# Starting the expert stage beside the routing of the last token tile

## The chip, the cores and the metric

The kernel runs on one core of a Trainium2 chip. The metric is device microseconds of one execution. Its engines work side by side and meet at semaphores: PE (TensorE, matrix products and transposes), DVE (VectorE), ACT (ScalarE), POOL (GpSimd) and SP, which here only issues transfers. POOL issues the transfers whose rows are picked by an index list (gathers and scatters). All transfers share 16 DMA engines.

## The reference, cut to what matters

One decoder layer over 1024 prompt tokens and 32 sample tokens: two kinds of attention, an output projection, then a mixture of 32 experts of which each token takes two.

```python
h = x + mixed @ w_out
f = hier_moe(rms_norm(h, g_ffn).reshape(B * T, -1), w_rg, b_rg, w_re, b_re, w_g, w_u, w_d)
return h + f.reshape(B, T, -1)

def hier_moe(x, ...):
    # group = argmax of 4 group logits; inside it the best 2 of 8 experts; gates sum to the group's probability
    ...
    hg = jnp.einsum('nd,edf->nef', x, w_g)
    hu = jnp.einsum('nd,edf->nef', x, w_u)
    act = jax.nn.silu(hg) * hu * dense_gate[..., None].astype(x.dtype)
    return jnp.einsum('nef,efd->nd', act, w_d)
```

All is float32. An expert's three matrices (1024x256 twice, 256x1024) are 3 MB. 1056 tokens with two experts each make 2112 rows of expert work.

## The kernel before, in words

Only the last third of the kernel is touched.

**Projection and routing, tile by tile.** Nine token tiles are taken in the list `order`: the 32 sample tokens (t = 8), then prompt tiles 0 to 7 of 128 tokens. `project(t)` loads the mixed attention output into a tile `mx` (L1311; the name has two buffers), rounds it on ACT into `mh` (L1313), subtracts on POOL so that `mx` holds the rest (L176), and makes two halves of 24 products (L1325 to L1327). The sum `h` goes to the output `y` (L1336) and to a scratch tensor `s_hn` (L1337). `route(t)` transposes `h`, makes 36 logits (L1354), and runs a long chain of small DVE instructions to two experts and a position for each token. Two small products (L1416) add the tokens to a PSUM table, `own`: 96 slots for each of 32 experts. Projection and routing of neighbouring tiles are woven together by generators, and the build system then lists the instructions of each engine in an order of its own, with semaphores where an operand or a buffer needs them.

**From table to slots.** After the last tile the table is copied (L1467), 12 small products turn it into 24 columns of 128 slots (L1473), and DVE writes `its`: token row, gate and norm factor of each slot (L1478 to L1480). The 3072 slots hold 2112 tokens; an empty slot points to a spare row behind the tokens. A few small DVE instructions behind that (to L1489) tell whether an expert overflowed; that path is not taken.

**Expert groups.** 24 groups of 128 slots, four units of 32 slots. For a group POOL gathers 128 rows of 4 KB from `s_hn` into `xg` (L1498, six buffers). PE transposes them (L1507, eight), DVE scales each half into `xT` (L1508), and PE makes the first products with `wg` (L1513; 64 instructions in the trace). ACT and DVE make the hidden values `ac` (L1519, L1522), PE transposes them (L1526, two), DVE copies them to `aTe` (L1528), and PE makes the second products with `wd` (L1533; 32 in the trace). ACT scales the result to `yo` (L1536), and POOL adds its rows to `y` (L1537). `down` of a group comes behind `gate_up` of the next.

**Weights.** SP loads `wg` (2 MB, two transfers, L1273) and `wd` (1 MB, L1266) into six buffers each. Experts 0 to 3 are loaded during projection, three more tiles at its end; the next wait for `its` (L1265, L1271), and all others for a buffer that PE has finished with.

Of the kernel before, what the change touches and what calls it, by code (L numbers as in the profile page):

```python
# [122 lines left out]
def build(tc, a, upto=99, dbg=None):  # L123
# [1181 lines left out]
    def project(t):  # L1305
# [36 lines left out]
    def route(t, h, s1):  # L1342
# [66 lines left out]
        for k in range(2):  # L1409
            V.tensor_tensor(out=ev[:, k], in0=oh[:n, k].unsqueeze(2).to_broadcast([n, 32, 3]),  # L1410
                            in1=val[:, k].unsqueeze(1).to_broadcast([n, 32, 3]), op=ALU.mult)
            V.tensor_tensor_reduce(out=j32, in0=pc[:n, :32], in1=oh[:n, k], op0=ALU.mult, op1=ALU.add, scale=1.0, scalar=0.0,
                                   accum_out=pos[:, k:k + 1])
            V.tensor_scalar(at[:, k], C("iota")[:n, :CAP], pos[:, k:k + 1], None, op0=ALU.is_equal)

            T_.matmul(T2[:CAP, :96], lhsT=at[:, k], rhs=ev[:, k].rearrange("p e u -> p (e u)"), start=t == order[0] and k == 0,  # L1416
                      stop=t == order[-1] and k == 1)

# [10 lines left out]
    def step(g):  # L1429
        next(g, None)  # L1430


# [6 lines left out]
    for i, t in enumerate(order):  # L1439
# [13 lines left out]
        if last:  # L1453
            step(last)
        if i == NT:

# [9 lines left out]
    ts = sm.tile([CAP, 32, 3], F32, name="ts", bufs=1)  # L1466
    V.tensor_copy(ts.rearrange("p e u -> p (e u)"), T2[:CAP, :96])  # L1467
    its = cq.tile([P, NSLOT // P, 3], I32, name="its")
    pi = low()[:, :3 * (NSLOT // P)].rearrange("p (m c u) -> p m c u", c=3, u=3)
    for u in range(3):  # L1470
        for b in range(4):
            r = (u - b) % 4
            T_.matmul(pi[32 * b:32 * b + 32, :, (3 * r + u) // 4, :], lhsT=ident[:CAP, 32 * u:32 * u + 32], rhs=ts[:, r::4, :],  # L1473
                      start=True, stop=True)
    pi = pi.rearrange("p m c u -> p (m c) u")

    em = sm.tile([P, NSLOT // P], F32, name="em", bufs=1)
    V.tensor_scalar(em, pi[:, :, 0], 0.0, C("prow1"), op0=ALU.is_equal, op1=ALU.mult)  # L1478
    V.scalar_tensor_tensor(its[:, :, 0], pi[:, :, 0], -1.0, em, op0=ALU.add, op1=ALU.add)
    V.tensor_copy(its[:, :, 1:].bitcast(F32), pi[:, :, 1:])  # L1480
    pc = low()
# [6 lines left out]
    V.tensor_scalar(cnti[:, 0:1], cnt[:, 32:33], float(P - 1 - CAP), None, op0=ALU.add)  # L1488
    V.tensor_scalar(cnti[:, 1:2], cnti[:, 0:1], 7, None, op0=ALU.arith_shift_right)  # L1489
    p3.close()  # L1490

# [3 lines left out]

    def fetch(it):
        xg = ep.tile([P, D], F32, name="xg", bufs=XG)
        G.indirect_dma_start(out=xg, out_offset=None, in_=hnd, in_offset=bass.IndirectOffsetOnAxis(ap=it[:, 0:1], axis=0))  # L1498
        return it, xg

    def gate_up(it, xg, units):

        xT = ep.tile([P, KC, P], F32, name="xT")
        for b in (0, 4):
            pt = tr()
            for k in range(b, b + 4):
# [9 lines left out]
    def down(it, gu, units):
        sg = ep.tile([P, 256], F32, name="sg")
        rs = it[:, 2:3].bitcast(F32)
        S.activation(sg, gu[:, :256], AF.Silu, scale=rs)  # L1519

        ac = ep.tile([P, 256], F32, name="ac")
        V.scalar_tensor_tensor(ac.rearrange("p (c n) -> p n c", c=2), gu[:, 256:].rearrange("p (n c) -> p n c", c=2), rs,  # L1522
                               sg.rearrange("p (n c) -> p n c", c=2), op0=ALU.mult, op1=ALU.mult)
        pt = tr()
        for k in range(2):
            T_.transpose(pt[:, k * P:(k + 1) * P], ac[:, k * P:(k + 1) * P], ident)  # L1526
        aT = ep.tile([P, 2, P], F32, name="aTe")
        V.tensor_copy(aT.rearrange("p k n -> p (k n)"), pt[:, :256])  # L1528
        py = big()
        for q in range(2):  # L1530
            for k in range(2):
                for c, m, (wg, wd) in units:
                    T_.matmul(py[c:c + m, q * 512:(q + 1) * 512], lhsT=aT[:, k, c:c + m], rhs=wd[:, k, q * 512:(q + 1) * 512],  # L1533
                              start=k == 0, stop=k == 1)
        yo = ep.tile([P, D], F32, name="yo", bufs=YO)
        S.activation(yo, py, AF.Copy, scale=it[:, 1:2].bitcast(F32))  # L1536
        G.indirect_dma_start(out=yd, out_offset=bass.IndirectOffsetOnAxis(ap=it[:, 0:1], axis=0), in_=yo, in_offset=None,  # L1537
                             compute_op=ALU.add)

    fetched = [fetch(its[:, g]) for g in range(2)]
    behind = None
    held = list(HOLD)
    for g in range(NSLOT // P):
        if g >= 2:
            fetched.append(fetch(its[:, g]))
        units = []
        for i in range(4):
            n = (4 * g + i) * 32 // CAP  # L1550
            for part in range(2):
                if (part, n) not in W_:
                    W_[(part, n)] = weights(8 * (n % 4) + n // 4, part, its[:, 0, 0:1] if held[part] > 0 else None)
                    held[part] -= 1

            units.append((32 * i, 32, (W_[(0, n)], W_[(1, n)])))
        ahead = gate_up(*fetched[g], units)
        if behind:
            down(*behind)
        behind = ahead  # L1560
    down(*behind)


    npass = nc.values_load(cnti[0:1, 1:2], min_val=0, max_val=8)
    with tc.If(npass > 0):
# [14 lines left out]
        with tc.For_i(0, 8, 1) as k:  # L1580
            with tc.For_i(0, 4, 1) as i:
                w = weights(i * 8 + k, 0), weights(i * 8 + k, 1)
                with tc.For_i(0, npass, 1) as q:
                    it = ep.tile([P, 3], I32, name="it")
                    Y.dma_start(it, tbl[bass.ds((k * 4 + i) * OVF + q * P, P)])
                    down(*gate_up(*fetch(it), [(0, P, w)]))
    p4.close()
# [39 lines left out]
```

## Time and profile before

| | us |
|---|---|
| median of 3 runs (lowest, highest) | 1397.38 (1395.25, 1399.51) |
| the profiled execution | 1403.95 |
| its span | 1402.1 |
| projection and routing of nine tiles, first product to last slot instruction | 931.8 to 1071.0 |
| 24 expert groups, first transpose to last product | 1079.3 to 1382.7 |

Times below are microseconds from the start of the profiled span. A row of the trace names the line of the kernel, the engine, the operation, what it writes and reads (`out<-in`), its form, and in brackets how long the engine stood idle ahead of it and what ended that. The trace counts each product twice (the lists of instructions show half as many), a transpose once. PE is busy 90% of the span and the DMA engines are nearly full through the expert stage, so a gain must be looked for in the places where PE stands idle.

### The profile page before, as it was taken

The page shows a single profiled execution, that of the slowest core. Times are in us where ns is not written, and L with a number is a line of the kernel's source. Part 1 is how long each engine was busy: PE and PEld are TensorE (multiplying, and loading weights), DVE is VectorE, ACT ScalarE, POOL GpSimd, SP SyncE. Part 2 cuts the span into 40 slices and gives each one's busy share as a digit, 9 for nine tenths or more (in the row PEclk, how much of TensorE's full clock was granted, in tenths as well). Part 3 has the DMA queues.
Part 4 walks back from the last instruction along what each step waited for, and adds up shares of the span by engine and source line. Part 5 has one row for each costly group of instructions (what it writes and reads, how often), then busy time and mean ns, then how long its engine had stood idle before and what let it go on. Part 6 is the DMA issues. An engine that isn't in the chain of part 4 may idle for free.

```text
span 1402.1 us, 24778 instructions
## 1 busy us (share of the span) xinstructions
PE 1265.0 (90%) x9359; PEld 855.0 (61%) x9359; DVE 792.0 (56%) x2218; ACT 561.5 (40%) x1239; POOL 447.8 (32%) x505
## 2 busy tenths in 40 slices
PE   7999999997799689898889989999996999999994
PEld 4877675875467576776675776768884333333341
DVE  5544996969987677766655556946754111111110
ACT  5533666895432365544345555732220111111110
POOL 1012233254336534435236544321212112222101
PEclk9999999998899899999899999999997999999997
DMA  6223004133325765666467654347657999999992
GB/s 234 77 88 109 25 24 121 48 109 82 90 97 147 227 244 213 234 210 230 152 227 252 222 161 148 103 135 306 247 172 256 341 370 377 377 381 386 378 340 47
DMA packets 114149, 279.92 MB, mean 200 GB/s; under 512 B 50664, under 2 KB 50920, under 8 KB 101736
## 3 DMA queue, kind: packets, MB, share of 16 engines
q1 hardware_dynamic: 81248, 180.84, 35.4%
q0 software_dynamic: 26272, 95.43, 21.8%
q10 hardware_dynamic: 6504, 2.01, 0.6%
q8 instruction: 75, 1.23, 0.3%
q14 instruction: 50, 0.41, 0.1%
HBM read 234.33 MB, written 43.92 MB: 198 GB/s over the span
## 4 chain that ended last, share of the span: by engine, by line
PE 44%; DMA 9%; DVE 6%; issue 5%; POOL 3%; ACT 2%; SPq 0%; another core or an unknown queue 0%; POOLq 0%; ACTq 0%; DVEq 0%
PE acc L1513 9%; PE S L1533 4%; DMA wg<-in_w_exp_up_dram 4%; PE tr L1104 4%; PE tr L876 3%; PE acc L1325 3%; PE acc L1326 2%; PE acc L1327 2%; PE tr L1112 2%; PE own L1165 2%; PE acc L978 2%; DMA wg<-in_w_exp_gate_dram 2%; PE acc L974 2%; PE tr L936 2%; PE tr L937 2%
## 5 line engine op out<-in xcount | busy, mean ns | idle before, releaser
L532 PE MATMUL acc<-wh,xh 128*128 128x512 f32 x432 | 174.9, 405 | 15.3 <-ACT wh L508 15.3
L1513 PE MATMUL acc<-wg,xT 128*32 128x512 f32 x1536 | 174.7, 598 | 2.8 <-DMA wg<-in_w_exp_up_dram 2.4
L533 PE MATMUL acc<-wh,xl 128*128 128x512 f32 x432 | 172.1, 398 | 0.0
L940 ACT ACTIVATE mk<-mk,mx 128x256 f32<-128x256 f32 (+7 forms) x128 | 99.0, 775 | 83.4 <-DVE mx L938 74.0
L535 PE MATMUL acc<-wl,xh 128*128 128x512 f32 x320 | 126.6, 396 | 0.0
L1513 PEld LDWEIGHTS acc<-wg,xT 128*32 128x32 f32 x1536 | 54.6, 110 | 104.2 <-issue 95.5
L532 PEld LDWEIGHTS acc<-wh,xh 128*128 128x128 f32 x432 | 82.4, 191 | 48.0 <-ACT wh L508 25.8
L1528 DVE COPY aTe<-tr 128x256 f32<-128x256 f32 x24 | 10.2, 425 | 162.6 <-PE tr L1526 162.6
L533 PEld LDWEIGHTS acc<-wh,xl 128*128 128x128 f32 x432 | 82.5, 191 | 17.4 <-issue 1.2
L1533 PE MATMUL S<-wd,aTe 128*32 128x512 f32 x768 | 87.5, 594 | 4.3 <-DVE aTe L1528 3.3
L1508 DVE TENSOR_TENSOR xT<-tr,gc 128x512 f32<-128x512 f32 x48 | 32.9, 688 | 91.5 <-PE tr L1507 91.5
L1104 PE MATMUL tr<-cst,pg 128*128 128x128 f32 x512 | 78.8, 286 | 0.5 <-DVE ql L407 0.4
L936 PE MATMUL tr<-KS,qh 128*128 128x512 f32 (+3 forms) x192 | 75.1, 396 | 1.6 <-DVE aT L864 0.8
L1519 ACT ACTIVATE sg<-acc,its 128x256 f32<-128x256 f32 x24 | 11.4, 474 | 156.0 <-PE acc L1513 156.0
L1537 POOL DMA_INDIRECT out_o_y_dram<-yo,its x24 | 38.0, 1582 | 110.2 <-ACT yo L1536 66.1
L958 POOL TENSOR_SCALAR mk<-mk,rl 128x128 f32<-128x128 f32 (+7 forms) x64 | 49.3, 781 | 70.9 <-DVE rl L950 65.8
L1498 POOL DMA_INDIRECT xg<-s_hn,its x24 | 23.4, 977 | 142.4 <-PE tr L1507 128.9
L876 PE MATMUL tr<-cst,mk 128*128 128x128 f32 x432 | 65.1, 281 | 4.0 <-POOL mk L958 2.4
L535 PEld LDWEIGHTS acc<-wl,xh 128*128 128x128 f32 x320 | 60.9, 190 | 11.8
L937 PE MATMUL tr<-KS,ql 128*128 128x512 f32 (+3 forms) x192 | 66.2, 359 | 0.0
L1536 ACT ACTIVATE yo<-S,its 128x1024 f32<-128x1024 f32 x24 | 26.8, 1115 | 98.5 <-PE S L1533 98.5
L1104 PEld LDWEIGHTS tr<-cst,pg 128*128 128x128 f32 x512 | 61.6, 147 | 6.5 <-issue 2.0
(416 smaller groups left out, 2924.2 us busy)
## 6 DMA issues: line engine op xcount, KB each, us to landing
wg<-in_w_exp_gate_dram SPq DMA_DIRECT2D x32, 1024.0 KB
wg<-in_w_exp_up_dram SPq DMA_DIRECT2D x32, 1024.0 KB
wd<-in_w_exp_down_dram SPq DMA_DIRECT2D x32, 1024.0 KB
wr<-in_w_in_dram SPq DMA_DIRECT2D x56, 256.0 KB
xt<-in_x_prompt_dram SPq DMA_DIRECT2D x16, 512.0 KB
s_mix<-mo SPq DMA_DIRECT2D x16, 256.0 KB
qn<-s_qa SPq DMA_DIRECT2D x8, 512.0 KB
raw<-in_w_out_dram SPq DMA_DIRECT2D x16, 256.0 KB
```

Source lines behind the costliest of these rows:

```text
L532: T_.matmul(ps, lhsT=xh[t][:, kc, :], rhs=wh[kc], start=kc == 0 and t < NT - 1, stop=False)
L533: T_.matmul(ps, lhsT=xl[t][:, kc, :], rhs=wh[kc], start=False, stop=t == NT - 1 and kc == KC - 1)
L535: T_.matmul(ps, lhsT=xh[t][:, kc, :], rhs=wl[kc], start=False, stop=kc == KC - 1)
L876: T_.transpose(pt[:, (j - b) * P:(j - b + 1) * P], src[:, j * P:(j + 1) * P], ident)
L936: T_.matmul(sp[:, :c1 - c0], lhsT=T.qh[:, h * P:(h + 1) * P], rhs=KS[:, h, c0:c1], start=True, stop=False)
L937: T_.matmul(sp[:, :c1 - c0], lhsT=T.ql[:, h * P:(h + 1) * P], rhs=KS[:, h, c0:c1], start=False, stop=True)
L940: S.activation(mk[:, :W], mk[:, :W], AF.Exp, bias=mx[:, h:h + 1], scale=-1.0, accum_out=T.ll[:, h:h + 1])
L958: G.tensor_scalar(ex[s][:, :W], ex[s][:, :W], T.rl[:, 2 * u + s:2 * u + s + 1], 1.0, op0=ALU.mult, op1=ALU.mult)
L1104: T_.transpose(pt[:, c * P:(c + 1) * P], raws[bb][:, o_:o_ + P], ident)
L1325: T_.matmul(ps[:n], lhsT=mh[:, k, :], rhs=woh[q][k], start=k == 0, stop=False)
L1513: T_.matmul(gu[c:c + m, :].rearrange("p (u f) -> p u f", u=2), lhsT=xT[:, k, c:c + m], rhs=wg[:, :, k, :], start=k == 0, stop=k == KC - 1)
L1533: T_.matmul(py[c:c + m, q * 512:(q + 1) * 512], lhsT=aT[:, k, c:c + m], rhs=wd[:, k, q * 512:(q + 1) * 512], start=k == 0, stop=k == 1)
```

## The change

Three edits.

*First group early.* When six prompt tiles and the sample tile are counted (before the last two tiles' counts; `EARLY = -2`), the table is copied once, the first 32 slots of experts 0, 1, 2 and 3 of the table's order are made into a group of their own, and the counts are raised so that later tokens of these experts take slots from 32 on. Its rows are gathered into a third tile of the name `mx`, between those of tiles 6 and 7. The transposes and first products of this group stand inside the routing of the last tile, and its second products behind the slots' instructions. Its hidden values and its result are kept in two tiles of the name `xt`. The last two tiles are counted in a second PSUM table, which is added to the first. The remaining groups run from 1 to 23; groups 1 and 2 hold the other slots of the first four experts.

*Empty slots not gathered.* The gather gets a bound (rows behind the tokens are left out), so the buffers must hold numbers: each of the six `xg` buffers is set to zero on DVE before its first gather. The last tile's `h` is written to `s_hn` ahead of `y`.

*Transposes of two groups together.* The two transposes of the hidden values of a group now stand with the eight of the next group, ahead of its first products.

```diff
-    T2 = own()
+    T2 = {0: own()}
+    EARLY = -2
...
+        for dst in ((hnd, yd) if t == order[-1] else (yd, hnd)):
+            st.dma_start(dst[r0:r0 + n], h[:n])
...
+    def fetch_to(it, xg):
+        G.indirect_dma_start(out=xg, out_offset=None, in_=hnd, in_offset=bass.IndirectOffsetOnAxis(ap=it[:, 0:1], axis=0),
+                             bounds_check=NTOK - 1, oob_is_err=False)
...
+    def early_slots():
+        V.tensor_copy(ts.rearrange("p e u -> p (e u)"), T2[0][:CAP, :96])
...
+        slots(it0, pi[:, :3].rearrange("p (g u) -> p g u", u=3))
+        xg0 = fp.tile([P, D], F32, name="mx")
+        V.memset(xg0, 0.0)
+        fetch_to(it0[:, 0], xg0)
...
+        if i == len(order) + EARLY:
+            early_slots()
...
-    for _ in range(3):
-        step(route_)
+    step(route_)
+    x0T = turn_rows(xg0s[0], lambda: fp.tile([P, KC, P], F32, name="mx"))
+    step(route_)
+    u0 = [(32 * i, 32, (W_[(0, i)], W_[(1, i)])) for i in range(4)]
+    gu0 = acc()
+    first_products(gu0, x0T, u0, 0, 4)
+    step(route_)
+    first_products(gu0, x0T, u0, 4, KC)
...
+    hid = fp.tile([P, D], F32, name="xt")
+    gated(it0[:, 0], gu0, hid[:, :256], hid[:, 256:512])
+    aT0 = hid[:, 512:768].rearrange("p (k n) -> p k n", k=2)
+    turn_hidden(hid[:, 256:512], aT0)
+    py0 = [acc(), acc()]
+    second_products(py0, aT0, u0)
+    yo0 = fp.tile([P, D], F32, name="xt")
+    for q in range(2):
+        S.activation(yo0[:, q * 512:(q + 1) * 512], py0[q], AF.Copy, scale=it0[:, 0, 1:2].bitcast(F32))
     p3.close()
...
+    def fetch(it, new=False):
         xg = ep.tile([P, D], F32, name="xg", bufs=XG)
+        if new:
+            V.memset(xg, 0.0)
+        fetch_to(it, xg)
...
+    fetched = {g: fetch(its[:, g], True) for g in (1, 2)}
+    add_rows(it0[:, 0], yo0)
+    behind = None
+    for g in range(1, NG + 2):
...
+            xT = turn_rows(xg, new_xT)
+        aT = turned_hidden(behind[1]) if behind else None
+        if g < NG:
+            gu = acc()
+            first_products(gu, xT, units, 0, KC)
         if behind:
-            down(*behind)
+            down(behind[0], aT, behind[2])
```

What this does to the order of instructions is seen at three places. In the lists, `[waits ...]` names the semaphores an instruction waits for: those of an engine, and DMAHW0 to 7 and DMASW0 to 7 for transfers issued by SP and by POOL, taken in turn.

The first place is SP's queue around the input of tile 7 (`mx` with the highest number; `out_o_y` and `s_hn` from the tiles `xt` of 4, 5 and 6 in turn). Before:

```order
L1311 DMA mx_11776<-s_mix 128x1024 [waits DMAHW1_49,PE_49,Pool_49]
L1336 DMA out_o_y_dram<-xt_11469 128x1024 [waits DMAHW2_49,DVE_49]
L1337 DMA s_hn<-xt_11469 128x1024 [waits DMAHW3_49]
L1318 DMA xt_11780<-in_x_prompt_dram 128x1024 [waits DMAHW2_49,DMAHW3_49,PE_49,Activation_49]
L1311 DMA mx_11929<-s_mix 128x1024 [waits DMAHW6_49,PE_49,Pool_49]
L1336 DMA out_o_y_dram<-xt_11622 128x1024 [waits DMAHW0_49,DVE_49]
L1337 DMA s_hn<-xt_11622 128x1024 [waits DMAHW7_49]
L1318 DMA xt_11933<-in_x_prompt_dram 128x1024 [waits DMAHW6_49,DMAHW7_49,PE_49,Activation_49]
L1336 DMA out_o_y_dram<-xt_11780 128x1024 [waits DMAHW4_49,DMAHW1_49,DVE_49]
```

And in the changed kernel, where L1314 is that load and L1341 both writes:

```order
L1341 DMA out_o_y_dram<-xt_11626 128x1024 [waits DMAHW1_49,DVE_49]
L1341 DMA s_hn<-xt_11626 128x1024 [waits DMAHW7_49]
L1321 DMA xt_11958<-in_x_prompt_dram 128x1024 [waits DMAHW6_49,DMAHW0_49,DMAHW7_49,PE_49,Activation_49]
L1314 DMA mx_11954<-s_mix 128x1024 [waits DMAHW2_49,PE_49,Pool_49]
L1341 DMA out_o_y_dram<-xt_11784 128x1024 [waits DMAHW5_49,DVE_49]
L1341 DMA s_hn<-xt_11784 128x1024
```

The load of `mx` for tile 7 stood ahead of tile 5's writes; it now stands behind them, directly ahead of tile 6's.

The second place is the start of the groups on POOL: `its` are the slots, `xt` with `it0` the result of the early group. Before:

```order
L1336 DMA out_o_y_dram<-xt_11933 128x1024 [waits DMAHW0_49,DMASW0_49,DVE_49]
L1337 DMA s_hn<-xt_11933 128x1024 [waits DMASW1_49]
L1340 TENSOR_TENSOR s1_11935<-s1_11935,nhalf_62 128x1 [waits DVE_49,Pool_49]
L1498 DMA xg_12206<-s_hn,its_12171 128x1024 [waits DMAHW2_49,DMASW2_49,DMAHW3_49,DMASW1_49,DMAHW4_49,DMASW0_49,DMAHW6_49,DVE_49,DMAHW7_49,PE_49,Activation_49]
L1498 DMA xg_12208<-s_hn,its_12171 128x1024 [waits DMASW3_49]
```

In the changed kernel, on POOL:

```order
L1449 DMA mx_11948<-s_hn,it0_10768 128x1024 [waits DMAHW4_49,DMAHW3_49,DMAHW6_49,DMAHW0_49,DMAHW7_49,DMASW0_49,DVE_49]
L1341 DMA s_hn<-xt_11958 128x1024 [waits DMASW1_49,DMAHW0_49,DMASW0_49,DVE_49]
L1341 DMA out_o_y_dram<-xt_11958 128x1024 [waits DMASW2_49]
L1344 TENSOR_TENSOR s1_11960<-s1_11960,nhalf_62 128x1 [waits DVE_49,Pool_49]
L1272 CAST wg_12467<-its_10767 128x1 [waits DMASW5_49,DMASW6_49,DVE_49,PE_49]
L1489 DMA out_o_y_dram<-xt_12304,it0_10768 1184x1024 [waits DMAHW2_49,DMAHW5_49,DMASW3_49,DMAHW6_49,DMASW2_49,Activation_49]
L1449 DMA xg_12316<-s_hn,its_10767 128x1024 [waits DMASW3_49,DMASW1_49,DMASW4_49,DVE_49,PE_49]
```

and on DVE:

```order
L1580 TENSOR_SCALAR cnti<-cnt 128x1 [waits DVE_49]
L1472 SCALAR_TENSOR_TENSOR xt<-acc,it_10768,xt 128x128x2 [waits DMAHW3_49,DMAHW2_49,Activation_49]
L1479 COPY xt<-tr 128x256 [waits PE_49]
L1599 MEMSET xg 128x1024 [waits DMASW2_49,DMASW3_49,DMASW1_49,Activation_49]
L1599 MEMSET xg 128x1024 x4
L1599 MEMSET xg 128x1024 [waits DVE_49,PE_49]
L1459 TENSOR_TENSOR xT<-tr,gc 128x512 [waits DMASW0_49,PE_49]
```

The scatter of the early group now stands ahead of the first gather by `its`, and that gather and the first clearing of an `xg` buffer both wait for the scatter's semaphore, DMASW3.

The third place is PE within the groups (`tr<-cst,xg` the eight transposes of a group's rows, `tr<-cst,ac` the two of its hidden values). Before:

```order
L1533 MATMUL S<-wd,aTe 32x512 x16
L1507 MATMUL tr<-cst,xg 128x128 x4
L1513 MATMUL acc<-wg,xT 32x512 x32
L1526 MATMUL tr<-cst,ac 128x128 x2
L1507 MATMUL tr<-cst,xg 128x128 x4
L1533 MATMUL S<-wd,aTe 32x512 x16
```

In the changed kernel:

```order
L1486 MATMUL S<-wd,aTe 32x512 x16
L1458 MATMUL tr<-cst,xg 128x128 x8
L1478 MATMUL tr<-cst,ac 128x128 x2
L1466 MATMUL acc<-wg,xT 32x512 x32
L1486 MATMUL S<-wd,aTe 32x512 x16
```

Four of the eight transposes stood between the hidden values' transposes and the second products; now all ten stand in one run ahead of the first products.

## Rows read from the trace of the kernel before

**Rows 1.** Busy time by stretch: us, PE, PEld, DVE, ACT, POOL, clock, DMA share, GB/s.

```profile
1062.00:1079.00 17.00, 3.84 (x42) 3.10 (x41) 7.25 (x52) 0.59 (x3) 4.11 (x5) 0.56 0.71 265
...
1275.00:1303.00 28.00, 26.33 (x219) 9.31 (x218) 5.15 (x9) 3.82 (x5) 5.16 (x4) 1.00 1.02 381
```

**Rows 2.** Chain that ended last, first two groups: start, duration, what.

```profile
1074.53 4.68 DMA xg<-s_hn,its
...
1079.26 1.97 PE tr L1507 x8
1081.23 8.59 PE acc L1513 x64
...
1102.94 0.64 PE tr L1507 x4
```

**Rows 3.** Waits from 1050 on: waiter, released by, total, times, longest.

```profile
PE acc L1513 <- DMA wg<-in_w_exp_up_dram: 2.4, 2, 2.2
```

**Rows 4.** Timeline of one expert group: start, duration, engine, line, what.

```profile
1188.64 0.71 PE L1507 MATMUL tr<-cst,xg 128*128 128x128 f32 x4
1189.28 7.07 PE L1513 MATMUL acc<-wg,xT 128*32 128x512 f32 x64
1189.39 0.69 DVE L1508 TENSOR_TENSOR xT<-tr,gc 128x512 f32<-128x512 f32 x1 [3.35 <-PE tr L1507]
...
1196.29 0.44 PE L1526 MATMUL tr<-cst,ac 128*128 128x128 f32 x2
...
1196.76 0.42 DVE L1528 COPY aTe<-tr 128x256 f32<-128x256 f32 x1 [6.68 <-PE tr L1526]
...
1197.33 3.64 PE L1533 MATMUL S<-wd,aTe 128*32 128x512 f32 x32 [0.16 <-DVE aTe L1528]
...
1200.90 0.71 PE L1507 MATMUL tr<-cst,xg 128*128 128x128 f32 x4
```

**Rows 5.** Waits of SP's queue, 960 to 1050.

```profile
SPq L1311 <- PE acc L1327: 15.4, 2, 8.8
```

**Rows 6.** Timeline of tile 7's input and products.

```profile
1030.18 0.32 SPq L1311 DMA_DIRECT2D mx<-s_mix  x1
...
1034.45 1.05 ACT L1313 CAST mh<-mx 128x1024 fp32r<-128x1024 f32 x1 [2.79 <-DMA mx<-s_mix]
...
1035.58 2.38 POOL L176 TENSOR_TENSOR mx<-mx,mh 128x1024 fp32r<-128x1024 f32 x1 [2.83 <-ACT mh L1313]
...
1044.87 0.48 PE L1325 MATMUL acc<-woh,mh 128*128 128x512 f32 x1
...
1058.62 0.39 PE L1326 MATMUL acc<-wol,mh 128*128 128x512 f32 x1
...
1058.84 0.39 PE L1327 MATMUL acc<-woh,mx 128*128 128x512 f32 x1
```

**Rows 7.** Busy time by stretch around an earlier idle gap of PE.

```profile
632.00:634.00 2.00, 0.00 (x0) 0.00 (x0) 0.73 (x4) 2.00 (x5) 0.00 (x0) 0.96 0.00 0
634.00:636.00 2.00, 1.62 (x8) 1.63 (x9) 1.12 (x3) 1.10 (x5) 0.00 (x0) 0.50 0.00 0
```

**Rows 8.** Timeline of the last counts and the slots.

```profile
1067.59 1.05 PE L1416 MATMUL own<-ev,at 128*96 128x96 f32 x4 [0.60 <-DVE at L1414]
...
1068.99 0.54 PE L1473 MATMUL low<-ts,cst 96*32 96x24 f32 x24 [0.35 <-DVE ts L1467]
...
1070.84 0.15 DVE L1489 TENSOR_SCALAR cnti<-cnti 128x1 int32<-128x1 int32 x1
```

**Rows 9.** Users of the slots, by instruction: times, ns min/median/max, first and last start, form.

```profile
L1522 DVE SCALAR_TENSOR_TENSOR ac<-acc,its,sg x24: 669/678/685, 1091.8 to 1374.2; 128x256 f32<-128x256 f32 x24
L1536 ACT ACTIVATE yo<-S,its x24: 1114/1114/1117, 1103.0 to 1382.7; 128x1024 f32<-128x1024 f32 x24
```

**Rows 10.** Chain that ended last: the scatter before the last.

```profile
1379.51 6.17 DMA out_o_y_dram<-yo,its
```

**Rows 11.** The clearing of a tile at line 780.

```profile
L780 DVE MEMSET xn<- x1: 912/912/912, 103.1 to 103.1; 128x1024 f32 x1
```

More of the change, by code (lines that the diff above doesn't have):

```diff
@@ L781, in build @@
     S.dma_start(hnd[NTOK:], zz)
+    S.dma_start(hnd[(NT - 1) * P:NT * P], zz)
     S.dma_start(a["o_y"][NTOK:], zz)
@@ new lines, in turn_rows, with first_products @@
+    def turn_rows(xg, new):
+        xT = new()
+        for b in (0, 4):
+            pt = tr()
+            for k in range(b, b + 4):
+                T_.transpose(pt[:, (k - b) * P:(k - b + 1) * P], xg[:, k::KC], ident)
+            V.tensor_tensor(out=xT[:, b:b + 4], in0=pt.rearrange("p (k n) -> p k n", n=P), in1=gc[:, b:b + 4].unsqueeze(2).to_broadcast([P, 4, P]),
+                            op=ALU.mult)
+        return xT
+    def first_products(gu, xT, units, k0, k1):
+        for k in range(k0, k1):
+            for c, m, (wg, wd) in units:
+                T_.matmul(gu[c:c + m, :].rearrange("p (u f) -> p u f", u=2), lhsT=xT[:, k, c:c + m], rhs=wg[:, :, k, :], start=k == 0, stop=k == KC - 1)
@@ new lines, in second_products, with add_rows @@
+    def second_products(py, aT, units):
+        for q in range(2):
+            for k in range(2):
+                for c, m, (wg, wd) in units:
+                    T_.matmul(py[q][c:c + m], lhsT=aT[:, k, c:c + m], rhs=wd[:, k, q * 512:(q + 1) * 512], start=k == 0, stop=k == 1)
+    def add_rows(it, yo):
+        G.indirect_dma_start(out=yd, out_offset=bass.IndirectOffsetOnAxis(ap=it[:, 0:1], axis=0), in_=yo, in_offset=None,
+                             compute_op=ALU.add)
+    its = cq.tile([P, NSLOT // P, 3], I32, name="its")
@@ new lines, in build @@
+    it0 = cq.tile([P, 1, 3], I32, name="it0")
+    ts = sm.tile([CAP, 32, 3], F32, name="ts", bufs=1)
+    xg0s = []
+    def early_slots():
+        V.tensor_copy(ts.rearrange("p e u -> p (e u)"), T2[0][:CAP, :96])
+        pc = low()
+        T_.matmul(pc[:, :4], lhsT=C("ones"), rhs=tot[:, :4], start=True, stop=True)
+        adj = sm.tile([1, 4], F32, name="adj", bufs=1)
+        V.tensor_scalar(adj, pc[0:1, :4], -1.0, 32.0, op0=ALU.mult, op1=ALU.add)
+        V.tensor_scalar(adj, adj, 0.0, None, op0=ALU.max)
+        V.tensor_tensor(out=tot[0:1, :4], in0=tot[0:1, :4], in1=adj, op=ALU.add)
+        pi = low()
+        for n in range(4):
+            T_.matmul(pi[32 * n:32 * n + 32, :3], lhsT=ident[:CAP, :32], rhs=ts[:, n, :], start=True, stop=True)
+        slots(it0, pi[:, :3].rearrange("p (g u) -> p g u", u=3))
+        xg0 = fp.tile([P, D], F32, name="mx")
+        V.memset(xg0, 0.0)
+        fetch_to(it0[:, 0], xg0)
+        xg0s.append(xg0)
@@ L1516, in down, with new_xT @@
[L1516 to L1519, printed above, removed]
-        ac = ep.tile([P, 256], F32, name="ac")
[L1522 to L1526, printed above, removed]
+    def new_xT():
+        return ep.tile([P, KC, P], F32, name="xT")
@@ L1527, in down, with hidden, turned_hidden @@
+    def hidden(it, gu):
+        ac = ep.tile([P, 256], F32, name="ac")
+        gated(it, gu, ep.tile([P, 256], F32, name="sg"), ac)
+        return ac
+    def turned_hidden(ac):
         aT = ep.tile([P, 2, P], F32, name="aTe")
-        V.tensor_copy(aT.rearrange("p k n -> p (k n)"), pt[:, :256])
+        turn_hidden(ac, aT)
+        return aT
+    def down(it, aT, units):
         py = big()
[L1530 to L1534, printed above, removed]
+        second_products([py[:, :512], py[:, 512:]], aT, units)
@@ L1535, in down, with units_of @@
         yo = ep.tile([P, D], F32, name="yo", bufs=YO)
         S.activation(yo, py, AF.Copy, scale=it[:, 1:2].bitcast(F32))
[L1537 to L1543, printed above, removed]
+        add_rows(it, yo)
+    NG = NSLOT // P
     held = list(HOLD)
-    for g in range(NSLOT // P):
-        if g >= 2:
-            fetched.append(fetch(its[:, g]))
+    def units_of(g):
```

76 lines of the change are left out of this document (42 added, 34 removed).

## The prediction

> **What bounds the kernel now.** I read the busy time by stretch first, then the chain that ended last, then the timeline of the places that the change touches. Between the last products of tile 7 and the first transpose of the groups PE is busy 3.8 of 17 us [rows 1]: it waits for the routing's small DVE instructions and then for the first gather. That is the hole in which the change puts a group. The chain shows what follows: gather of 4.68 us, transposes from 1079.26, slow first products (8.59 us), and by 1102.94 the first products of groups 0 and 1 and the second products of group 0 are done [rows 2]. This point, "first products of two groups and second products of one", exists in both kernels, and I compare them there. From then on PE waited for weights only 2.4 us in all [rows 3] and sets the pace, one group in 12.26 us (1188.64 to 1200.90) [rows 4], while the DMA engines are full (share 1.02, 381 GB/s) [rows 1]. So PE and the weights are close to level, and both must be followed.
>
> **Tile 7 starts later.** The name `mx` has two buffers. The load for tile 7 could start at 1030.18 because it needed the buffer of tile 5 (SP waits there for products of an earlier tile) [rows 5, 6]. The early group's rows now take that buffer, so tile 7 needs tile 6's, and its load stands directly ahead of tile 6's writes in SP's queue. Tile 6's last products end where tile 7's first product starts, at 1044.87. From load to cast took 4.27 us (1030.18 to 1034.45), from cast to POOL's start 1.13, POOL 2.38 [rows 6]: the rest is ready at 1044.87 + 0.1 + 7.8 = 1052.8. Four of the 48 products need only `mh` and can go ahead; the other 44 take 0.23 us each (1058.62 to 1058.84) [rows 6], with four transposes 10.6 us, so tile 7 ends at 1063.4 instead of 1059.1: 4.3 us late. In the gap PE has only scraps to do (counts, logits of tile 6, slots of the early group). After an idle gap of 2.6 us the clock went from 0.96 to 0.50, which is the lower level of 1.2 GHz [rows 7]; if that happens here, some 3.5 us of products cost double, 1.75 us. I take half: **5.2 us**, bounds 4.3 and 6.1. Below 4.3 it could go only if the load came sooner.
>
> **The last routing is longer.** Two DVE multiplications of 0.69 us [rows 4] for the early group stand ahead of the last tile's logits, 1.2 us after overlap. Behind the last count products (1067.59, 1.05 us) [rows 8] now stand 11 listed first products, 22 in the trace, at 7.0/64 us each 2.4 us, in which the 0.35 us for copying the table is hidden; and 24 instead of 12 slot products add 0.5 us (0.54 for the old 12, 24 in the trace [rows 8]). The other first products lie under the DVE chain and cost nothing; if the clock is low there, they outgrow that cover by about 1 us. **3.7 us**, bounds 3.0 and 4.7. The last slot instruction ends about 1070.84 + 8.9 = 1079.7 instead of 1070.84 [rows 8].
>
> **The start of group 1 hangs on a longer chain.** Before, it was 8.42 us from 1070.84 to the first transpose at 1079.26, the gather [rows 2, 8]. Now the scatter of the early group stands ahead of that gather on POOL, and the clearing of the first buffer waits for the scatter to land, because the buffer lies where the early result lay. Step by step: hidden values 0.68 [rows 9], two transposes until the copy 0.48 and copy 0.42, second products 3.57 (1197.33 to 1200.90) [rows 4], half of the 1.11 for the result [rows 9] with its hop 0.7, scatter 6.17 with 0.27 ahead of it [rows 10], clearing 0.91 [rows 11], gather 4.68 [rows 2], five hops of 0.15 (as 0.16 ahead of the second products [rows 4]). That is 18.6. At the low clock the second products take 7.1; PE was idle in pieces before, I take 5.0: **20.0 us**, bounds 18.1 and 22.6. The first transpose is then at 1099.7. Queued behind the waiting clearing on DVE are five more clearings (4.6 us), done while the gather runs, and behind the scatter on POOL all gathers, which nobody needs sooner than the first. PE idles over 10 us, as before, so transposes and first products again cost 1.97 + 8.59: the point of comparison is at 1110.3, against 1102.94, **7.3 us late**. One group of 12.26 us has been done in the hole, but what was put behind it costs more.
>
> The Trainium skill (DMA: Bandwidth & Descriptors, "Anatomy of one DMA — SWDGE (gpsimd) path") fits such a transfer as 2.0 us plus its bytes over 436 GB/s; an estimate from it for 512 KB is 3.2 us. The rows have 6.17 for the scatter and 4.68 for the gather [rows 2, 10]; by the page the start would be 4.5 us sooner and the whole sum 4.5 less. The sum goes by the rows.
>
> **One run of ten transposes.** The old order had a stall-free cycle: four transposes of the next group lie under the copy of the hidden values. In the new one the transposes of the hidden values need a PSUM buffer (two of that name), which the first DVE multiplication must leave. It starts 0.75 us behind the first transpose and takes 0.69 [rows 4], so with a hop the two transposes start at 1.55 instead of 0.9 us. They take 0.21, and 0.21 more pass until products run (four transposes and that take 0.64, 1188.64 to 1189.28). So a group is 1.97 + 7.01 + 3.57 = 12.55 us, 0.29 more than 12.26. 22 groups follow the point of comparison: **6.4 us**. Without the stall it would be 0.4 less than before, 22 groups 8.8 us less; with a hop or two more, 9 us more. I take 0.29, worked out from the nearest rows.
>
> **Weights and gathers.** 960 of 3072 slots are empty; not gathering them saves 3.9 MB, 10 us of full DMA engines, if the transfer is really left out. Against it, the buffers of the first experts come free late: experts 0 and 1 only at the point of comparison, where before two loads of 2 MB had started. At that point about 2.6 MB more of weights are to come, and 17 gathers of 0.36 MB instead of 15 of 0.52, net 0.8 MB or 2 us: the stream runs 9.3 us late. At the place where PE waited before, 16 groups on, PE is 7.3 + 16 x 0.29 = 11.9 us late, so it no longer waits: **2.4 us less**. The new writes of zeros stand at the start, near 104 us, and cost nothing; bounded by 1.4 us (512 KB at 381 GB/s).
>
> **The sum.** 7.3 + 6.4 - 2.4 = 11.3 us more. Against the profiled execution of 1403.95 that is 1415.2; that execution is 6.6 above the median of the runs, and the same difference on the median 1397.38 gives **1408.7 us**, 0.8% slower.
>
> **The rivals.** *The early group is free.* The load of tile 7 is not held up, and group 1's gather follows the slots as before. Then 5.2 goes, and the chain is 8.4: first transpose at 1070.84 + 3.7 + 8.4 = 1083.0, comparison point 9.4 us early, and with +6.4 and -2.4 the sum is -5.4: 1392.0. It speaks for it that both engines have the room; against it that both waits stand in the lists of instructions. It decides by the first transpose of group 1: only if it is before about 1088 can the kernel be faster.
>
> *The groups get shorter, and the weights set the pace.* If no stall comes and a group takes 11.86, PE would be 0.9 us late where it waited before, but the stream is 9.3 late. PE waits there for the difference and wins 0.4 in each of the last six groups: 9.3 - 2.4 = 6.9, 1404.3. For it: full DMA engines over the whole stage. Against it: the buffer and the multiplication.
>
> *The empty rows cost as much as before.* The gathers left are then 17 of 0.52 MB, the stream has 3.6 MB more to move, 9.5 us, and is 16.8 us late where PE is 11.9 late. It waits, and six groups of +0.29 follow: 18.5, 1415.9. The trace of before has no gather with rows left out, so nothing excludes it.
>
> **How the numbers follow.** Forecast 0.60, early group free 0.12, weights set the pace 0.18, empty rows cost 0.10. The forecast's own range is 1402 to 1415, from the bounds of its terms. For 8 in 10 over all cases I reach half into the fast rival and up to the last one: 1395 to 1417. About 0.3% (4.2 us) is what a measurement of this kernel can tell from no change. Slower by more than that: 0.52 of the forecast, 0.10 of the second rival, 0.10 of the third, 0.72. Same: 0.07, 0.08 and 0.02 of the first rival, 0.17. Faster: 0.10 of the first rival and 0.01, 0.11.
>
> **What would show it.** Right: the load of tile 7's `mx` issued near 1045 and a gap of some 6 us in PE before tile 7's products; the last slot instruction near 1080; the first clearing of `xg` just behind the scatter's landing; first transpose of group 1 near 1100; about 0.6 us of PE idle ahead of each pair of transposes of hidden values; no wait of PE for weights. Wrong, step by step: the load near 1030; a first transpose before 1092; groups of 12.0 us or less; PE waits for `wg` in several groups (then the weights set the pace, and the lead or the lag at the start decides by its bytes).

## The result and the profile after

| | kernel before | changed kernel |
|---|---|---|
| median of 5 runs (lowest, highest), us | 1395.25 (1393.59, 1399.51) | 1409.41 (1406.60, 1412.98) |
| the profiled execution, its span | 1403.95, 1402.1 | 1406.6, 1404.8 |
| ratio, 95% interval | | 1.0095 (1.0076, 1.0115) |

The change makes the kernel slower by 1.0%: 14.2 us between the medians, 13.3 us by the ratio, with an interval of 10.6 to 16.0. The forecast was 11.3 us more and, from a median of 1397.38, 1408.7. The two profiled executions differ by less than the medians, since the one of before is 8.7 us above its median, the one after is 2.8 below its own, and the one of before reached the stretch that the change touches 9.4 us later. So I count from a point that both have: the end of tile 6's products, where DVE starts to add their second half (1044.71 before, 1035.34 after).

| us from the end of tile 6's products | before | after | later by | forecast |
|---|---|---|---|---|
| tile 7's products end | 14.6 | 19.3 | 4.8 | 5.2 |
| slots copied | 25.6 | 33.3 | 7.7 | 8.9 |
| first transpose of group 1 | 34.6 | 54.8 | 20.2 | 20.4 |
| first products of two groups and second of one | 58.2 | 65.6 | 7.4 | 7.3 |
| end of the span | 357.4 | 369.5 | 12.1 | 11.3 |

The timeline of the changed kernel from tile 7's input to the early group's second products (start, duration, engine, line, what; in brackets the idle time ahead and what ended it) answers to [rows 6]:

```profile
1035.34 0.69 DVE L1333 TENSOR_TENSOR xt<-acc,xt 128x512 f32<-128x512 f32 x1 [1.92 <-PE acc L1330]
1035.37 0.32 SPq L1314 DMA_DIRECT2D mx<-s_mix  x1
...
1039.47 1.04 ACT L1316 CAST mh<-mx 128x1024 fp32r<-128x1024 f32 x1 [2.62 <-DMA mx<-s_mix]
1040.65 2.37 POOL L176 TENSOR_TENSOR mx<-mx,mh 128x1024 fp32r<-128x1024 f32 x1 [2.53 <-ACT mh L1316]
...
1043.07 0.80 PE L1330 MATMUL acc<-woh,mx 128*128 128x512 f32 x1 [0.40 <-POOL mx L176]
...
1054.67 0.69 DVE L1333 TENSOR_TENSOR xt<-acc,xt 128x512 f32<-128x512 f32 x1 [4.87 <-PE acc L1330]
...
1068.63 0.20 DVE L1445 COPY its<-low 128x48 f32<-128x48 f32 x1
...
1070.99 5.34 PE L1486 MATMUL acc<-wd,xt 128*32 128x512 f32 x32 [0.52 <-DVE xt L1479]
```

The load goes out the moment tile 6's products end, where before it went out 14.5 us ahead of that. From load to first product with the rest: 7.7 us. The busy time by stretch (columns as in [rows 1]) has the clock at the end of this gap, where tile 7's products begin (0.66), the clock in the next gap (0.50), and two stretches at the end of the groups:

```profile
1040.00:1045.00 5.00, 4.60 (x19) 3.36 (x19) 3.92 (x17) 1.11 (x4) 3.50 (x2) 0.66 0.24 97
1080.00:1085.00 5.00, 0.00 (x0) 0.00 (x0) 0.91 (x1) 0.00 (x0) 0.00 (x0) 0.50 0.51 92
1278.00:1303.00 25.00, 24.32 (x218) 8.37 (x210) 4.83 (x9) 3.18 (x4) 4.45 (x4) 1.00 1.02 378
1303.00:1328.00 25.00, 20.65 (x167) 6.72 (x168) 2.33 (x4) 1.59 (x2) 3.11 (x2) 0.93 1.02 391
```

The chain that ended last, from the early group's scatter to the point of comparison (start, duration, what), answers to [rows 2]:

```profile
1077.38 6.30 DMA out_o_y_dram<-xt,it
...
1084.05 0.92 DVE xg L1599
...
1085.75 4.35 DMA xg<-s_hn,its
...
1090.14 1.97 PE tr L1458 x8
1092.12 8.82 PE acc L1466 x64
```

Scatter, clearing, gather, transposes, products, each waiting for the one ahead: from the slots' copy (1068.63) to the first transpose it is 21.5 us, where it was 8.9. PE stands still for 13.8 us of it. Last, PE's waits over the whole span (waiter, released by, total, times, longest), to set beside [rows 3]:

```profile
PE tr L1458 <- DMA xg<-s_hn,its: 13.8, 1, 13.8
...
PE tr L1478 <- DVE xT L1459: 7.8, 22, 0.8
...
PE acc L1466 <- DMA wg<-in_w_exp_up_dram: 5.3, 2, 4.0
```

The wait for weights, which the forecast had gone, has grown from 2.4 to 5.3. What it costs is seen best on ACT, which starts `sg` once a group:

```profile
1297.08 0.47 ACT L1470 ACTIVATE sg<-acc,its 128x256 f32<-128x256 f32 x1 [7.73 <-PE acc L1466]
...
1316.02 0.47 ACT L1470 ACTIVATE sg<-acc,its 128x256 f32<-128x256 f32 x1 [14.37 <-PE acc L1466]
```

These two are 18.94 us apart, and nearly all others 12.30. What such intervals (all above 12.5) have over 12.30, summed, I call the kernel's *pauses*: 5.1 us before, 9.0 after. They are more than the waits in the list. Behind the longer wait, for example, the clock is lower (0.93 over 1303 to 1328) and 57 products take 8.25 us, where 64 take 7.00 in other groups.

### The profile page after: what moved, and what is told of

It reads as the page before. It is cut to its first block, busy times and chain, and to the rows that moved or that the text cites. A ratio compares the mean times of both kernels' runs of the same rounds, so it can differ in the third digit from the quotient of the medians.

```text
span 1404.8 us, 24868 instructions
## 1 busy us (share of the span) xinstructions
PE 1260.7 (90%) x9393; PEld 842.3 (60%) x9393; DVE 801.0 (57%) x2232; ACT 561.9 (40%) x1240; POOL 449.8 (32%) x505
## 3 DMA queue, kind: packets, MB, share of 16 engines
q0 software_dynamic: 26272, 91.50, 21.3%
## 4 chain that ended last, share of the span: by engine, by line
PE 43%; DMA 9%; DVE 7%; issue 5%; POOL 4%; ACT 3%; SPq 0%; POOLq 0%; ACTq 0%; DVEq 0%
PE acc L1466 9%; PE S L1486 4%; PE tr L1105 3%; PE tr L877 3%; PE tr L1113 3%; PE acc L1328 3%; PE acc L1330 2%; PE acc L1329 2%; PE acc L979 2%; DMA wg<-in_w_exp_up_dram 2%; DMA wg<-in_w_exp_gate_dram 2%; DMA wd<-in_w_exp_down_dram 2%; PE acc L975 2%; PE tr L938 2%; PE tr L937 2%
## 5 line engine op out<-in xcount | busy, mean ns | idle before, releaser
L532 PE MATMUL acc<-wh,xh 128*128 128x512 f32 x432 | 174.4, 404 | 14.2 <-ACT wh L508 14.2
L1466 PE MATMUL acc<-wg,xT 128*32 128x512 f32 x1472 | 168.1, 604 | 5.3 <-DMA wg<-in_w_exp_up_dram 5.3
L1472 DVE SCALAR_TENSOR_TENSOR ac<-acc,its,sg 128x256 f32<-128x256 f32 x23 | 15.9, 691 | 174.2 <-ACT sg L1470 174.2
L1466 PEld LDWEIGHTS acc<-wg,xT 128*32 128x32 f32 x1472 | 46.3, 111 | 110.2 <-issue 107.6
L1459 DVE TENSOR_TENSOR xT<-tr,gc 128x512 f32<-128x512 f32 x46 | 29.7, 685 | 60.9 <-PE tr L1458 60.9
L340 POOL TENSOR_TENSOR m<-raw,gtab 128x512 f32<-128x512 f32 x32 | 47.6, 1486 | 49.2 <-ACT raw L377 36.2
```

Source lines behind the costliest of these rows:

```text
L340: last_rot[0] = (V if n == NS else G).tensor_tensor(out=m2[:n, :w].rearrange('p (h u d) -> p h u d', u=2, d=32), in0=sv[:, :, ::-1, :], in ...
L532: T_.matmul(ps, lhsT=xh[t][:, kc, :], rhs=wh[kc], start=kc == 0 and t < NT - 1, stop=False)
```

## The experiments

Absolute times differ by 2% between the chips on which these ran (the kernel before took 1373 to 1400 us), so each is given as its ratio to the kernel before on the same chip, with the 95% interval; where us are told, they are the difference of two ratios times 1395.25. The pauses are those of one profiled execution; e8 and e11 are the same kernel, and theirs are 0 and 5.0, so a difference of some us in that column shows nothing without the ratio beside it.

| run | ratio | interval | pauses, us |
|---|---|---|---|
| changed kernel | 1.0095 | 1.0076 to 1.0115 | 9.0 |
| e1, tile 7's load first | 1.0064 | 1.0046 to 1.0082 | 9.0 |
| e2, result elsewhere | 1.0061 | 1.0044 to 1.0078 | 10.0 |
| e3, group 1's rows first | 0.9998 | 0.9985 to 1.0011 | 10.4 |
| e4, e1 and e3 | 0.9964 | 0.9951 to 0.9977 | 11.0 |
| e5, before, gathers bounded | 0.9990 | 0.9971 to 1.0008 | 1.6 |
| e6, before, transposes together | 0.9998 | 0.9979 to 1.0016 | 3.5 |
| e7, changed, no bound | 1.0129 | 1.0107 to 1.0152 | 12.3 |
| e8, e4 with scatters bounded | 0.9917 | 0.9897 to 0.9938 | 0 |
| e9, e5 with scatters bounded | 0.9968 | 0.9956 to 0.9981 | 0 |
| e10, changed, scatters bounded too | 1.0042 | 1.0027 to 1.0056 | 0 |
| e11, e8 again | 0.9911 | 0.9891 to 0.9932 | 5.0 |
| e12, changed, scatters bounded instead | 1.0049 | 1.0034 to 1.0064 | 2.6 |

**The start: e1 to e4.**

```diff
  e1: early_slots() one step later, behind the first step of tile 7's project()
+        if i == len(order) + EARLY + 1:
+            early_slots()
```

> Edit: the early group's rows take their `mx` buffer after tile 7 has taken its own, so tile 7's input needs tile 5's buffer, as before the change. Theory (the start of the expert stage is lost in two places, this buffer and the scatter ahead of group 1's gather, and what is lost there is lost at the end): tile 7's `mx` is loaded before tile 6's products end, tile 7's products end about 14.6 us after tile 6's instead of 19.3, every later point 4.8 us sooner, the whole 1409.4 - 4.8 = 1404.6 us. Rival (the weights' stream sets the end, the start has slack): tile 7 sooner by the same, but PE waits longer for `wg` later on and the whole stays within 2 us of 1409.4.

Measured: 4.3 us less than the changed kernel. SP's queue issues tile 7's load at 1000.47, and tile 6's and tile 7's products end 15.4 us apart (14.6 before, 19.3 after); the pauses are unchanged. So 3.9 of the 4.8 us hang on the buffer, and a gain of that size reaches the end. Rows of e1's timeline:

```profile
1000.47 0.32 SPq L1314 DMA_DIRECT2D mx<-s_mix  x1
...
1015.14 0.69 DVE L1333 TENSOR_TENSOR xt<-acc,xt 128x512 f32<-128x512 f32 x1 [1.93 <-PE acc L1330]
...
1030.57 0.69 DVE L1333 TENSOR_TENSOR xt<-acc,xt 128x512 f32<-128x512 f32 x1 [2.13 <-PE acc L1330]
```

```diff
  e2: the yo buffers take the place at the pool's start
+    ep.tile([P, D], F32, name="yo", bufs=YO)
     fetched = {g: fetch(its[:, g], True) for g in (1, 2)}
```

> Edit: the four `yo` buffers are placed first in their pool, so they and not an `xg` buffer lie over the early group's result; the scatter stays ahead of the gather on POOL. Theory: the first clearing of `xg` no longer waits for the scatter to land; group 1's gather is issued right behind the scatter (about 10 us after the slots), and the first transpose comes about 15 us after the slots' last instruction instead of 21.5: 6.4 us sooner, 1409.4 - 6.4 = 1403.0. Rival (the gather needs what the scatter's place on POOL and the full DMA engines give it, or the weights' stream sets the end): gather's landing takes several us longer than 4.35, or the gain is waited off at `wg`: 1407 to 1409.

Measured: 4.7 us less. The clearings run at once, the gather stands right behind the scatter's issue, and the first transpose comes 14.8 us after the slots' copy (1052.99), as expected, 6.7 us sooner. The difference between 6.7 and 4.7 us is inside the interval; the pauses are 1 us longer in this execution. Rows of e2's timeline:

```profile
1052.99 0.20 DVE L1445 COPY its<-low 128x48 f32<-128x48 f32 x1
...
1055.46 0.91 DVE L1599 MEMSET xg<- 128x1024 f32 x1 [0.16 <-issue]
...
1060.05 1.71 POOL L1489 DMA_INDIRECT out_o_y_dram<-xt,it  x1 [6.65 <-ACT xt L1589]
...
1062.06 1.06 POOL L1449 DMA_INDIRECT xg<-s_hn,its  x1 [0.30 <-DVE xg L1599]
...
1067.80 1.97 PE L1458 MATMUL tr<-cst,xg 128*128 128x128 f32 x8 [8.80 <-DMA xg<-s_hn,its]
```

```diff
  e3: e2, and behind the slots, ahead of the early group's hidden values
+    xg1 = fp.tile([P, 8, P], F32R, name="mh").rearrange("p c n -> p (c n)").bitcast(F32)
+    V.memset(xg1, 0.0)
+    fetch_to(its[:, 1], xg1)
...
-    fetched = {g: fetch(its[:, g], True) for g in (1, 2)}
+    fetched = {1: (its[:, 1], xg1), 2: fetch(its[:, 2], True)}
```

> Edit: as in e2, and group 1's rows go to a free `mh` buffer, cleared early and gathered right behind the slots, ahead of the early group's hidden values and its scatter. Theory: first transpose of group 1 about 9 us after the slots' last instruction (as in the kernel before: 9.03) instead of 21.5, 12.5 us sooner: 1397 us, level with the kernel before. Rival (PE is then busy with the early group's second products, low clock, or the weights' stream sets the end): less than half of it, 1403 or more.

Measured: 13.5 us less, level with the kernel before. Rows of e3's timeline:

```profile
1047.27 0.20 DVE L1445 COPY its<-low 128x48 f32<-128x48 f32 x1
1047.65 1.11 POOL L1449 DMA_INDIRECT mh<-s_hn,its  x1 [11.12 <-DVE cnt L1576]
...
1054.91 0.71 PE L1458 MATMUL tr<-cst,mh 128*128 128x128 f32 x4
1055.78 0.71 PE L1458 MATMUL tr<-cst,mh 128*128 128x128 f32 x4 [0.16 <-ACT xt L1592]
1056.01 1.64 POOL L1489 DMA_INDIRECT out_o_y_dram<-xt,it  x1 [7.04 <-ACT xt L1592]
1056.42 7.07 PE L1466 MATMUL acc<-wg,xT 128*32 128x512 f32 x64
```

The first transpose now follows the early group's second products without an idle gap, 7.6 us after the slots' copy, and the scatter leaves later; PE waits 0.7 us for group 2's gather, which stands behind it on POOL. More came than was expected: since PE did not stand still ahead of it, eight transposes and 64 products take 8.6 us (1054.91 to 1063.5) and not the 10.8 of the changed kernel (1090.14 to 1100.94), where the clock was 0.50 in the gap ahead.

> Edit: e1 and e3 together. Theory: the two losses add, 4.8 + 12.5 = 17.3 us, 1392 us, 3 us faster than the kernel before (0.998 of it), and the point where the first products of two groups and the second products of one are done comes about 48 us after tile 6's products end (58.4 before the change, 65.6 after it). Rival (weights' stream): the point comes as early, but PE then waits for `wg` for more than 10 us in all, and the whole is 1398 or more.

Measured: 18.3 us less than the changed kernel, and faster than the kernel before by 0.36%. The point of comparison comes 45.7 us after tile 6's products (65.6 changed, 58.2 before); a clearing on DVE holds up their addition here, so the count starts at the clearing, 1016.9. The losses add (4.3 and 13.5 us alone), with the 2.2 us of faster products among them; the pauses are 2 us longer in this execution. PE's waits in e4:

```profile
PE tr L1478 <- DVE xT L1459: 7.4, 22, 0.3
...
PE acc L1466 <- DMA wg<-in_w_exp_up_dram: 6.6, 3, 2.6
```

**The two other edits alone: e5 and e6.**

```diff
  e5: in the kernel before
-    def fetch(it):
+    def fetch(it, new=False):
         xg = ep.tile([P, D], F32, name="xg", bufs=XG)
+        if new:
+            V.memset(xg, 0.0)
         G.indirect_dma_start(out=xg, ..., in_offset=bass.IndirectOffsetOnAxis(ap=it[:, 0:1], axis=0),
+                             bounds_check=NTOK - 1, oob_is_err=False)
```

> The kernel before with only the empty slots not gathered (bound on the gather, six clearings; the last tile's write order as before). Theory (rows left out are not moved, and the weights' stream gains what they would have taken): software queue 3.93 MB less, the wait of PE for `wg` (2.4 us, some 4 us with the clock behind it) gone, one clearing of 0.9 us more ahead of the first gather: 1 to 3 us faster, 0.998 to 0.999 of before. Rival (a row left out costs the engines as much as one that is moved): as before or 1 us slower, the wait stays.

Measured: 0.9990, with 1 inside the interval. In its trace the wait for `wg` is down to one of 0.7 us and the pauses from 5.1 to 1.6. That rows left out are not moved is shown by the software queue's row (packets, MB, share):

```profile
q0 software_dynamic: 26272, 91.50, 21.2%
```

It has 3.93 MB less than before (95.43), which is 960 rows of 4 KB, in the same number of packets.

```diff
  e6: in the kernel before, gate_up() of a group makes the two transposes of the group behind
+        aT = turned(behind) if behind else None
         gu = acc()
         for k in range(KC):
```

> The kernel before with only the order of PE changed: the two transposes of hidden values stand with the eight of the next group. The step of the prediction said +0.29 us a group, 23 groups: +6.7 us, 1.0048 of before. Theory now (the cycle in the trace after is 12.30 against 12.26: the stall of 0.34 is paid back by second products of 3.43 instead of 3.57 and by fewer breaks): +0.04 a group, +0.9 us, within 0.2% of before. Third way (the stall vanishes here): 0.4 less a group, 0.993.

Measured: no difference. Not +6.7 us, as the prediction's step has it. PE's waits in e6, and under them the matching row of the kernel before:

```profile
PE tr L1531 <- DVE xT L1508: 7.1, 21, 0.3
...
PE S L1541 <- DVE aTe L1533: 0.6, 1, 0.6
```

```profile
PE S L1533 <- DVE aTe L1528: 3.3, 15, 0.6
```

The new order has its stall of 0.34 in each group. But the old one, which the prediction called free of stalls, had one too: 15 times 0.22 us ahead of the second products, until `aTe` was copied.

**The weights: e7 to e12.**

```diff
  e7: in the changed kernel
     def fetch_to(it, xg):
         G.indirect_dma_start(out=xg, ..., in_offset=bass.IndirectOffsetOnAxis(ap=it[:, 0:1], axis=0),
-                             bounds_check=NTOK - 1, oob_is_err=False)
  e8, e10: in add_rows(), on e4 and on the changed kernel; e9: on e5; e12: on e7
         G.indirect_dma_start(out=yd, ..., in_=yo, in_offset=None,
+                             bounds_check=NTOK - 1, oob_is_err=False,
                              compute_op=ALU.add)
```

> The changed kernel without the bound on the gather: empty slots fetch their spare rows as before the change; all else as changed. Theory (after the change the weights' stream is what PE waits for at the end, and the bound spares it 3.93 MB, 10 us at 381 GB/s): PE waits for `wg` some 10 us longer than 5.3, the whole 8 to 10 us slower than the changed kernel, ratio to before about 1.016. Rival (the groups set the pace, the stream has slack, or a row left out costs as much): ratio 1.009 to 1.010, wait as in the changed kernel.

Measured: in the direction of the theory, but smaller: the pauses grow by 3.3 us, the ratio by 0.0034, and the intervals of the two ratios overlap. The 10 us were mis-sized: the 3.93 MB came back (95.43 MB in the queue's row), but less than half of the time.

> e4 with a bound on the scatters too: empty slots' rows are not added to the spare rows behind the tokens, which nobody reads. Theory (the stream is what PE waits for at the end of e4, 6.6 us): 960 rows of 4 KB less to move, at least 3.9 MB or 10 us of full DMA engines, so the wait for `wg` goes and what it costs with it: 4 to 7 us faster than e4, ratio to before 0.991 to 0.9935. Rival (the groups set the pace, the waits are only a shift): ratio 0.996 as e4.

Measured: 0.9917, 6.6 us less than e4, at the upper end of what was expected. In its profiled execution PE waits for `wg` no more, and 3.93 MB less are moved.

> The kernel before with empty slots left out of the gathers (as e5) and of the scatters; no early group. What is asked: how much of e8's 0.9917 needs the early group. Theory (two separate gains: PE waits less for `wg`, 5.1 us of pauses in the trace of before, 1.6 left in e5; and the early group in its hole, worth 10 us at the point of comparison once nothing holds it up): 0 to 1 us of pauses for `wg`, ratio 0.996 to 0.998. Rival (the bounds alone are the gain): 0.992.

Measured: 0.9968, no pauses. So the bounds alone bring 0.3%, and the early group, with nothing in its way, 0.5% more (e8, e11; the joined transposes, which e8 has too, changed nothing in e6).

> The changed kernel with the bound on its scatters too; the start is left as changed. Theory (the changed kernel loses 7.2 us at the point of comparison and 9.0 us to pauses at `wg`, of which the kernel before has 5.1): the pauses go, the loss at the start stays: 6 to 9 us faster than the changed kernel, ratio to before 1.003 to 1.005. Rival (the pauses are only the late start handed on, and go back to it): ratio 1.0095 as the changed kernel.

Measured: 1.0042, no pauses, 7.4 us less than the changed kernel. Beside e9, which has no pauses either, it is 0.74% or 10.3 us slower; the start (7.4) and the cycle (0.9) make 8.3 of it, and the rest lies inside the intervals. The start and the pauses are two separate losses. The order of the last tile's two writes, also part of the change, was not varied.

> e8 once more beside the two others, on their chip: ratio to before 0.9917 again (0.9897 to 0.9938). In the profile of e8 ACT's first values of group 1 came 3.1 us after the products' end, as in no other run; if that belongs to the kernel it is here again, and the median has it in it; if it was one execution's, the first two groups are 17.3 us apart, as in e4.

Measured: 0.9911. The first two groups are 17.3 us apart, so the 3.1 us of e8's profile were that execution's. Here one wait for `wg` of 2.6 us is left, which e8's profiled execution, late by those 3.1 us from its first groups on, did not have:

```profile
PE acc L1466 <- DMA wg<-in_w_exp_up_dram: 2.6, 1, 2.6
```

> The changed kernel with the bound on its scatters instead of its gathers: the same 960 rows of 4 KB are left out, on the other side. Open is why leaving rows out of the scatters too took away 9.0 us of pauses (e10) and leaving them out of the gathers 3.3 (e7 against the changed kernel). Theory (a scattered row costs the stream more than a gathered one: 6.2 to 6.3 us against 4.4 to 4.7 for 128 rows): the software queue moves 91.5 MB as in the changed kernel, pauses at `wg` 3 to 4 us, ratio to before 1.004 to 1.007. Rival (only the bytes count): pauses 9 us, ratio 1.009 to 1.010.

Measured: 1.0049 with the bytes of the changed kernel (91.51 MB), pauses 2.6: the theory. The same 200 us of the span in the changed kernel and in e12, by busy time:

```profile
1100.00:1300.00 200.00, 192.88 (x1705) 67.12 (x1696) 37.90 (x65) 24.79 (x32) 40.56 (x32) 1.00 1.01 375
```

```profile
1100.00:1300.00 200.00, 193.00 (x1708) 67.90 (x1704) 37.36 (x64) 25.39 (x32) 38.94 (x30) 1.00 1.02 393
```

With the DMA engines as full (1.01, 1.02) they move 393 GB/s instead of 375. In e12's execution the groups start 19.3 us sooner; over the same groups (1080.7 to 1280.7) its engines move 389 at a share of 1.01. The ratios agree: for the same bytes e12 is 0.46% faster than the changed kernel, and the intervals lie apart. In this kernel, an empty row that is scattered holds the weights up longer than one that is gathered.

## Why the prediction was right, and where it was not

**Right: tile 7, the routing, the chain.** Each wait is where the lists of instructions had put it. e1 takes the first away and gets 4.3 us of 4.8 back; e3 takes the second away and gets 13.5. The slots came 1.2 us sooner than forecast: the last routing was longer by 2.9 us and not by 3.7. The chain made up for it. Its second products took 5.34 us, between the 3.57 and the 7.1 of the bounds; scatter and gather took 6.30 and 4.35 against the 6.17 and 4.68 of [rows 2, 10]. The estimate of 3.2 us from the Trainium skill (DMA: Bandwidth & Descriptors, "Anatomy of one DMA — SWDGE (gpsimd) path") is too short for both; the measurement decides.

**Wrong in size: ten transposes in one run.** The step took 1.97 + 7.01 + 3.57 = 12.55 us for a group; it is 12.30, 0.04 over the old cycle, 0.9 us for 22 groups instead of 6.4. One cycle in the changed kernel's chain, to set beside [rows 4]:

```profile
1113.58 0.66 PE tr L1458 x4
...
1114.26 0.70 DVE xT L1459
...
1115.01 0.44 PE tr L1478 x2
1115.44 7.00 PE acc L1466 x64
1122.45 3.43 PE S L1486 x32
1125.88 0.66 PE tr L1458 x4
```

The mechanism is there: the chain goes from the first transposes over DVE's first multiplication, and the two transposes wait 0.34 us for it. But 7.01 and 3.57 were read from the old order, where transposes and a copy stand between first and second products. In the new one the second follow the first without a break, and both together take 10.44 us (1115.44 to 1125.88): 0.14 less. The other 0.11 is the start of the cycle, 1.86 and not 1.97. The 3.3 us of waits shown under e6 are not the 0.14: they stand ahead of the second products, which take the same behind a short and behind a longer wait for the copy, as the chain of before has it:

```profile
1098.82 0.44 DVE aTe L1528
1099.30 3.64 PE S L1533 x32
...
1123.16 0.44 DVE aTe L1528
1123.73 3.64 PE S L1533 x32
```

Those waits are also inside the 12.26 from which the 0.29 was reckoned. So the wait that the edit adds came close to its price (the two transposes start 1.50 us behind the first one, forecast 1.55, though PE is idle for only 0.34 of that and not for 0.6); what failed are the durations around it, which were read beside other neighbours than they have now. Why products behind a break take longer, no run shows.

**Wrong in sign: PE no longer waits for weights.** The step had PE 11.9 us late where it waited before, behind a stream 9.3 us late. Of the 11.9 the cycle was to give 16 x 0.29 = 4.6; with 0.04 PE is only 8 us late, the stream is not, and PE waits. By the prediction's own numbers that is 9.3 - 8.0 = 1.3 us more waiting, not 2.4 less; the wait grew by 2.9 and the pauses by 3.9. The rest goes back to the 9.3, which was too small. The longest wait of before and of after is for the same load, that of group 18:

```profile
1276.20 27.69 DMA wg<-in_w_exp_up_dram
1304.03 7.03 PE acc L1513 x58
```

```profile
1278.98 28.19 DMA wg<-in_w_exp_up_dram
...
1307.30 8.25 PE acc L1466 x57
```

Counted from tile 6's products PE goes on at 259.3 before and at 272.0 after, so the stream is 12.6 us late there, 4.6 more than PE's 8.0 and near the 3.9 of the pauses. In e7, which gathers the empty rows, it is 16.2 us, near the 16.8 of the third rival: the bound spares the stream 3.5 us there, where the prediction's bytes made it 7.5. (Each is one execution.) This is the second rival's place, met halfway, and in part the third's. e10 and e12 show that it is the stream: with less to move the pauses go or shrink, and e10, without pauses, keeps the start's loss.

**The sum.** Forecast 7.3 + 6.4 - 2.4 = 11.3; measured 7.4 + 0.9 + 3.9 = 12.2, of which the traces show 12.1. That lies inside the 10.6 to 16.0 of the runs. But the sum came out better than its terms: 6.4 was 5.5 too high and -2.4 was 6.3 too low. Part of this belongs together, since each us that PE gains on the late stream comes back as waiting for weights (3.7 of the 6.3 by the prediction's own numbers). The rest is luck: the stream's lateness was set 3.3 us too low, which had nothing to do with the cycle. Luck too is that 1408.7 is within 1 us of 1409.41, since it starts from a median 2.1 us above that of the five runs. The early group itself is worth its place (e8 against e9: 0.5%), but not behind these two waits.

## What to carry to other kernels

Work that is moved into a hole takes buffers and a place in queues with it: look up who had that buffer next, and what the first instruction behind it in memory now waits for, before you count the hole as won. When you price a new order with durations of the old one, look at what stood on either side of them there: the same products were 0.14 us a group shorter without a break between them. Where two engines are close to level, a term that shortens one of them is worth only the distance to the other.

## What was not expected of the hardware

Rows that an indirect transfer leaves out stay in the packet count (26272 in all kernels) but not in the bytes (95.43, 91.50, 87.58 MB). Leaving 960 rows out of the scatters took 9.7 us off the pauses (12.3 in e7 to 2.6 in e12), out of the gathers 3.3 (to 9.0), for the same 3.93 MB. By the ratios it is 11.2 us against 4.7, of which only the first is clear of the intervals. Whether adding costs more for any row, or because the empty rows of all groups are added to the same few spare rows, was not tried and stays open.
